# Six row pairs in place of seven by seven block products in a decoder layer's second feed-forward network, and a modulation slab's dot products moved

## The chip, the cores and the metric

The kernel runs on one core of a Trainium2 chip. The metric is the device time of one execution in microseconds. Before the change the median of three runs is 566.43 us (566.12 to 567.93).

## The reference, cut to what matters

One decoder layer over 256 tokens of width 1024, with a conditioning vector `c`: a feed-forward network, token mixing, a second feed-forward network and a final norm. All is float32.

```python
mod = c_act @ w_ada[l] + b_ada[l]
sh1, sc1, g1, sh2, sc2, g2, sh3, sc3, g3 = jnp.split(mod, N_MOD, axis=-1)
...
u = modulate(rmsnorm(h, norm_ff2[l]), sh3, sc3)
h = h + FFN_RES * g3[:, None, :] * swiglu(u, w_ff2_gate[l], w_ff2_up[l], w_ff2_down[l])
return rmsnorm(h, norm_final)
...
def swiglu(x, w_gate, w_up, w_down):
    return (jax.nn.silu(x @ w_gate) * (x @ w_up)) @ w_down
```

`w_ada` gives nine modulation slabs of 1024 columns each; the last, slab 8, is the gate `g3`. The hidden width is 2816, which is 22 blocks of 128.

## The kernel before

**Products.** Each float32 operand is split in two: ScalarE rounds it to a high part (`hi`), VectorE subtracts that from it (`lo`), and TensorE forms each product in three matmuls (high by high, high by low, low by high). Weight tiles are 128 by 1024. SP loads them into eight buffers (`raw`) in turn, so a load is issued when the tile eight places back has been read for the last time. The split parts have six buffers each (`hi`, `lo`). Every engine carries out its instructions in the order in which the program issues them (`InOrder`).

**The second feed-forward network** runs over the hidden blocks f0 to f21. *Step f n* (`gate_up`) makes block n: 48 matmuls of 256 columns, 24 for the gate and 24 for the up weights, into one PSUM bank; then ScalarE takes the silu (`sg`), VectorE the *product* with the up half (`m`), and both split it into the rows (`s`) that the down product reads. `Pipe.run` issues these two instructions and the splits of the next weight tiles behind the matmuls of the following step, so that five split tiles (`AHEAD4`) are kept ready.

**The down product** takes hidden blocks in pairs: *pair n* is f2n and f2n+1. A plain pair (`down`) has 48 matmuls of 256 columns. A pair in `QUARTERED` is instead multiplied as two by two blocks by Strassen's and Winograd's scheme, with seven block products (`sevenths`): the *first products* of pair n are three, issued behind step f2n+2, and the *last products* four, issued behind f2n+3. Each has three matmuls of 512 columns. Their seven sums stay in seven of the eight PSUM banks (`qbanks`) over all pairs. The scheme needs sums of weight blocks, which VectorE makes in two more `raw` tiles (`quarters`: one combination of 512 columns with the first tile, three with the second) and splits as well, and sums of hidden rows (`Halved.steps`, tile `wide`). Behind the last quartered pair VectorE puts the seven sums together (`put_together`, tile `of_token`), and 16 transposes bring the result into the accumulators of the plain pairs, which follow: the pairs ahead of `QUARTERED` through `down`, then pairs 9 and 10, which close the sum.

**The modulation slabs.** One *slab step* (`AdaQueue.step`) loads two tiles of `w_ada` and takes two dot products of 1024 columns on VectorE; four steps make a slab, and `ada_close` then adds the bias. `SLAB_AT` names the jobs behind which the four steps of slab 8 are issued: `("f", n)` is step f n, `(0, n)` and `(1, n)` are the first and the last products of pair n. Behind the last one, `as_row` writes two columns of the gate to DRAM and reads them back as a row over all partitions, by two DMAs of GpSimd (`rbs_dram`, `rbs`), and the same for the final norm's gain (`gqk`). The weight tiles of pairs 9 and 10 are multiplied by that row when they have been loaded (`Stream.load`, `raw<-raw,rbs`).

Of the kernel before, what the change touches and what calls it, by code (L numbers as in the profile page):

```python
# [30 lines left out]
LED = "g0 g0 g1 g0 g1 A g2 g4 g2 g3 g1 g2 g3 A g4 g3 g5 g6 g5 g7 g6 g4 g7 g6 g7 g5"  # L31
Q1_AT = (2, 4, 6, 7, 7, 10, 11, 11, 13, 16, 16, 17, 18, 22)
Q2_AT = (4, 9, 13)
SLAB_AT = ("f", 3), ("f", 4), (1, 4), (1, 7)
QUARTERED = range(2, 9)
HALF = 4 * P + 32
SW = S + 2
UP = 320
# [69 lines left out]
def hybrid_layer(ctx: ExitStack, tc: tile.TileContext, first, xT, tri_d, mask_d, rel_bias,  # L108
# [61 lines left out]
    def row(shape=(P, S), dt=F32, tag="r1", bufs=6):  # L170
        return wk.tile(list(shape), dt, tag=tag, name=name(tag), bufs=bufs)
# [54 lines left out]
    def mm(out_ap, bank_t, lhsT, rhs, stop=False):  # L226

        first = id(bank_t) not in opened
        i = ten.matmul(out_ap, lhsT, rhs, start=first, stop=stop, skip_group_check=True)
        last_mm[0] = i  # L230
        if first:
            opened[id(bank_t)] = (i, bank_t)
        else:
            tc.add_manual_dep(i.ins, opened[id(bank_t)][0].ins.name, DEP, reason="the bank's first matmul")
        return i
# [250 lines left out]
    def gated(b, t):  # L486

        sg = row(tag="sg", bufs=3)
        act.activation(sg, b[:, 0:S], AF.Silu)
        yield  # L490
        m = row(tag="m", bufs=3)
        vec.tensor_tensor(out=m, in0=sg, in1=b[:, S:2 * S], op=ALU.mult)
        yield
        split_rows(t[:, 0, :], t[:, 1, :], m)
        yield
# [20 lines left out]
    class Halved:  # L516
# [11 lines left out]
        def add(self, b, i=None):  # L528
            i = self.n if i is None else i
            self.n = max(self.n, i + 1)  # L530
            return self.steps(b, i) if i // 2 in QUARTERED else gated(b, self.place(i))

# [55 lines left out]
    def sevenths(n, todo, banks, hid):  # L588

        def run():  # L590
            ws = [stream.take() for _ in range(2)]
            for i, rows, w, half in todo:
                if i not in banks:
                    banks[i] = bank()
                for part, r in ((0, 0), (0, 1), (1, 0)):
                    mm(banks[i], banks[i], hid.at[n][rows][:, r], ws[w][part][:, half * HALF:half * HALF + 4 * P],
                       stop=(n == QUARTERED[-1] and part == 1))

        return run
# [15 lines left out]
    def gate_up(hid, u):  # L615
        def run():
            b = bank()
            for c in range(2):
                one_by_one(b, c * S, stream.take(), u)
            return lambda: all_of(hid.add(b))  # L620

        return run

    def down(n, banks, hid):
        def run():
            ws = [stream.take() for _ in range(2)]
            if not banks:
                banks.extend(bank() for _ in range(5))
            for j in range(KD):
                down_block(j, ws, banks, hid.tiles[n])  # L630

        return run
# [201 lines left out]
    for f in range(NF):  # L834
        stream.unit(("gu2", f), gu2[f])
        work2.append(("f", f))
        n, second = divmod(f - 2, 2)
        if n in QUARTERED:
            if not second:
# [3 lines left out]
    for n in range(NF // 2):  # L843
        if n not in QUARTERED:
            stream.unit(("dn2", n), dn2[n])
# [499 lines left out]
    def as_row(src, tag, bufs):  # L1345
        there, t = dr.tile([2, P], F32, name=f"{tag}_dram"), row(tag=tag, bufs=bufs)
        nc.gpsimd.dma_start(there.rearrange("i p -> p i"), src)
        nc.gpsimd.dma_start(t, bass.AP(tensor=there.tensor, offset=there[:, :].offset, ap=[[0, P], [1, 2 * P]]))
        return t
# [3 lines left out]
    def put_together():  # L1353
        of_token.extend([mid([P, D]), mid([P, D])])
        b, (u2, u3), (lo, hi) = qbanks, [row((P, 512), tag="wide", bufs=2) for _ in range(2)], (slice(0, 512), slice(512, D))
        act.activation(u2, b[1], AF.Copy)
        for to, x, y, op in ((of_token[0][:, lo], u2, b[2], ALU.add), (u2, u2, b[6], ALU.add),
                             (u3, u2, b[7], ALU.add), (of_token[1][:, lo], u3, b[4], ALU.subtract),
                             (of_token[1][:, hi], u3, b[5], ALU.add), (u2, u2, b[5], ALU.add),
                             (of_token[0][:, hi], u2, b[3], ALU.add)):  # L1360
            vec.tensor_tensor(out=to, in0=x, in1=y, op=op)

    for what, n in work2[3:]:
        pipe.run(gate_up(hid, u3) if what == "f" else sevenths(n, SEVENTHS[what], qbanks, hid))
        if (what, n) in SLAB_AT:
            slabs.step()
        if (what, n) == SLAB_AT[-1]:
            stream.gains, nf = as_row(mods[:, 8, 6:8], "rbs", 1), row((P, 8), tag="tiny", bufs=4)
            vec.tensor_copy(nf[:, :2], colt[:, C_NF + 6:C_NF + 8])
            nf_row = as_row(nf[:, :2], "gqk", 4)  # L1370
        if (what, n) == (1, QUARTERED[-1]):
            put_together()
# [3 lines left out]
    for t, js in ((0, range(4)), (1, range(4)), (1, range(4, 8)), (0, range(4, 8))):  # L1376
        for j in js:
# [4 lines left out]
            opened.setdefault(id(b), (x, b))  # L1382
    for n in range(QUARTERED[0]):
        pipe.run(down(n, dbanks, hid))
# [197 lines left out]
```

## Time and profile before

| | before |
|---|---|
| median of three runs | 566.43 us |
| profiled execution, its time | 569.2 us |
| profiled execution, span | 567.4 us |
| ScalarE busy | 317.2 us (56%) |
| GpSimd busy | 17.9 us (3%) |
| bytes moved | 141.99 MB, mean 250 GB/s |
| chain that ended last, TensorE's share | 84% |
| the same, VectorE's share | 10% |

A profile's rows give the start in microseconds from the span's start and the duration, then the engine (PE is TensorE, DVE VectorE, ACT ScalarE, POOL GpSimd, SP SyncE; a q behind it means its instruction queue), the operation, what it writes and reads by the program's tile names, and the shape. Almost all instructions have line 133, since a helper issues them. In brackets stands how long the engine was idle before, and which engine and tile released it. A row with xN joins N instructions.

### The profile page before, as it was taken

Reading aid. Unit: us, or ns where it says so; the run is one execution under the profiler, and the core shown is the slowest. Engines: PE = TensorE matmul, PEld = TensorE weight load, DVE = VectorE, ACT = ScalarE, POOL = GpSimd, SP = SyncE. Lnnn points to the kernel's source line nnn. Section 1 sums busy time; section 2 is a strip of 40 time slices with the busy share of each in tenths; the row PEclk is TensorE's granted clock in tenths of the full one; section 3 lists DMA queues with packets and bytes.
Section 4 is the critical chain, followed back from the end, with each engine's and each line's share of the span. In section 5 each row is a group of like instructions: output and inputs, shape, how many; then the busy total and the mean of one; then the engine's idle time right before and its main releaser. Section 6 shows DMA issues by size and latency. Waiting matters only on the chain.

```text
span 567.4 us, 11461 instructions
## 1 busy us (share of the span) xinstructions
PE 552.8 (97%) x4531; PEld 537.8 (95%) x4531; DVE 485.4 (86%) x781; ACT 317.2 (56%) x531; POOL 17.9 (3%) x39
## 2 busy tenths in 40 slices
PE   7999999999999999999999999999899989998996
PEld 6999999999999999989999999999898979997996
DVE  6999897888887896999999888899888998987845
ACT  5557754444444678944955344676465554663524
POOL 1000030000000100000010000000000000001000
PEclk9999999999999999999999999999999989998999
DMA  8999799999998446545597879817746665659602
GB/s 326 409 408 408 236 354 392 407 342 344 322 383 263 152 142 230 176 151 181 191 351 293 319 263 305 261 39 236 246 154 219 197 219 177 216 191 216 215 2 74
DMA packets 40541, 141.99 MB, mean 250 GB/s; under 512 B 4740, under 2 KB 6248, under 8 KB 40488
## 3 DMA queue, kind: packets, MB, share of 16 engines
q1 hardware_dynamic: 39720, 139.55, 70.9%
q0 software_dynamic: 336, 0.80, 0.5%
q10 hardware_dynamic: 432, 0.92, 0.5%
q8 instruction: 35, 0.57, 0.4%
q14 instruction: 18, 0.15, 0.1%
HBM read 140.19 MB, written 1.06 MB: 249 GB/s over the span
## 4 chain that ended last, share of the span: by engine, by line
PE 84%; DVE 10%; issue 3%; ACT 1%; DMA 1%; POOL 0%; POOLq 0%; DVEq 0%; SPq 0%; ACTq 0%
PE b L133 84%; DVE lo L133 4%; DVE raw L133 3%; DVE m L133 1%; DMA b<-in_first 1%; DVE wide L133 1%; DVE s L133 1%; DVE n L133 1%; DVE ub L133 0%; ACT s L133 0%; ACT hi L133 0%; DVE sg L133 0%; ACT sg L133 0%; POOL tiny L435 0%; POOLq L1577 0%
## 5 line engine op out<-in xcount | busy, mean ns | idle before, releaser
L133 PE MATMUL b<-ub,hi 128*128 128x256 f32 (+1 forms) x1920 | 323.6, 280 | 5.7 <-DVE m L133 5.7
L133 PEld LDWEIGHTS b<-ub,hi 128*128 128x128 f32 x1920 | 284.5, 190 | 8.9 <-DVE m L133 7.9
L133 DVE TENSOR_TENSOR lo<-raw,hi 128x1024 fp32r<-128x1024 f32 (+2 forms) x204 | 236.3, 1192 | 31.4 <-ACT hi L133 30.8
L133 PE MATMUL b<-ub,lo 128*128 128x256 f32 (+1 forms) x960 | 246.6, 278 | 0.0
L133 ACT ACTIVATE hi<-raw 128x1024 fp32r<-128x1024 f32 (+2 forms) x204 | 202.3, 1029 | 39.8 <-DMA raw<-in_first 16.0
L133 PEld LDWEIGHTS b<-ub,lo 128*128 128x128 f32 x960 | 172.7, 190 | 0.0
L133 PE MATMUL b<-s,hi 128*128 128x256 f32 x720 | 123.5, 276 | 0.0
L133 PEld LDWEIGHTS b<-s,hi 128*128 128x128 f32 x720 | 108.4, 188 | 0.0
L133 PE MATMUL b<-s,lo 128*128 128x256 f32 x360 | 99.4, 276 | 0.0
L133 ACT ACTIVATE s<-m 128x256 fp32r<-128x256 f32 (+1 forms) x52 | 20.8, 403 | 104.6 <-DVE m L133 104.6
L133 DVE SCALAR_TENSOR_TENSOR raw<-raw,cact 128x1024 f32<-128x1024 f32 (+1 forms) x64 | 75.8, 1219 | 0.0
L133 PEld LDWEIGHTS b<-s,lo 128*128 128x128 f32 x360 | 67.6, 188 | 0.0
L133 ACT ACTIVATE sg<-b 128x256 f32<-128x256 f32 x46 | 17.1, 379 | 39.9 <-PE b L133 38.9
L133 PE MATMUL b<-hi,s 128*128 128x512 f32 (+1 forms) x114 | 34.1, 385 | 1.7 <-ACT s L133 1.1
L133 DVE TENSOR_TENSOR s<-m,s 128x256 fp32r<-128x256 f32 (+1 forms) x52 | 20.9, 405 | 16.5 <-ACT s L133 16.3
L133 PEld LDWEIGHTS b<-hi,s 128*128 128x128 f32 x114 | 19.8, 190 | 5.6 <-ACT s L133 1.5
L133 ACT ACTIVATE s<-b 128x512 f32<-128x512 f32 (+5 forms) x38 | 14.7, 437 | 17.6 <-PE b L133 16.7
L133 DVE TENSOR_TENSOR m<-sg,b 128x256 f32<-128x256 f32 x43 | 17.7, 416 | 5.1 <-ACT sg L133 5.0
L133 PE MATMUL b<-lo,s 128*128 128x512 f32 (+1 forms) x57 | 21.4, 387 | 0.0
L133 PE MATMUL b<-hi,ub 128*128 128x264 f32 (+1 forms) x96 | 16.7, 322 | 0.0
L133 ACT ACTIVATE sq<-b 128x256 f32<-128x256 f32 x24 | 9.1, 406 | 11.4 <-DVE b L133 9.3
L133 DVE SCALAR_TENSOR_TENSOR b<-b,mods,b 128x256 f32<-128x256 f32 x24 | 10.4, 478 | 5.9 <-PE b L133 5.9
(152 smaller groups left out, 361.2 us busy)
## 6 DMA issues: line engine op xcount, KB each, us to landing
raw<-in_gu SPq DMA_DIRECT2D x72, 512.0 KB, 5.5
raw<-in_ada SPq DMA_DIRECT2D x56, 512.0 KB, 5.8
raw<-in_dn SPq DMA_DIRECT2D x44, 512.0 KB, 6.7
raw<-in_win SPq DMA_DIRECT2D x24, 512.0 KB, 4.5
raw<-in_first SPq DMA_DIRECT2D x16, 513.0 KB, 8.3
raw<-in_first SPq DMA_DIRECT2D x16, 512.0 KB, 8.1
raw<-in_gbr SPq DMA_DIRECT2D x16, 512.0 KB, 6.4
raw<-in_wout SPq DMA_DIRECT2D x8, 512.0 KB, 5.5
```

The source lines that it names most:

```text
L133: x = getattr(self.engine, op)(*args, **kw)
```

## The change

The first quartered pair is 3 in place of 2: six pairs are left, and pair 2 becomes a third plain pair in front of pairs 9 and 10. The four steps of slab 8 stand behind f3, f5, f20 and f21 in place of f3, f4, pair 4's last products and pair 7's last products. `as_row` goes with the last of them.

```diff
-SLAB_AT = ("f", 3), ("f", 4), (1, 4), (1, 7)
-QUARTERED = range(2, 9)
+SLAB_AT = ("f", 3), ("f", 5), ("f", 20), ("f", 21)
+QUARTERED = range(3, 9)
```

On VectorE ahead of the quartered pairs, from the split behind product f3 on, there stand before (`raw<-raw` without a second input is a weight combination, `raw,gemv` a dot product of a slab step):

```order
L133 TENSOR_TENSOR lo_5303<-raw_5300,hi_5302 128x2x512
L133 TENSOR_TENSOR raw_5310<-raw_5306 128x512
L133 TENSOR_TENSOR lo_5313<-raw_5306,hi_5312 128x512
L133 SCALAR_TENSOR_TENSOR raw_5316,gemv<-raw_5316,cact 128x1024
L133 SCALAR_TENSOR_TENSOR raw_5319,gemv<-raw_5319,cact 128x1024
L133 TENSOR_TENSOR m_5373<-sg_5371,b_5245 128x256
L133 TENSOR_TENSOR s_853_5375<-m_5373,s_853_5375 128x128
L133 TENSOR_TENSOR raw_5310<-raw_5308,raw_5310 128x512
L133 TENSOR_TENSOR raw_5378<-raw_5308,raw_5306 128x512
L133 TENSOR_TENSOR raw_5378<-raw_5310,raw_5308 128x512
L133 TENSOR_TENSOR lo_5383<-raw_5308,hi_5382 128x2x512
L133 TENSOR_TENSOR lo_5389<-raw_5386,hi_5388 128x2x512
```

and of the change at the same place:

```order
L133 TENSOR_TENSOR lo_5303<-raw_5300,hi_5302 128x2x512
L133 TENSOR_TENSOR lo_5309<-raw_5306,hi_5308 128x2x512
L133 TENSOR_TENSOR m_5364<-sg_5362,b_5245 128x256
L133 TENSOR_TENSOR s_847_5361<-m_5364,s_847_5361 128x256
L133 TENSOR_TENSOR lo_5371<-raw_5368,hi_5370 128x2x512
L133 TENSOR_TENSOR lo_5377<-raw_5374,hi_5376 128x2x512
L133 SCALAR_TENSOR_TENSOR raw_5380,gemv<-raw_5380,cact 128x1024
L133 SCALAR_TENSOR_TENSOR raw_5383,gemv<-raw_5383,cact 128x1024
L133 TENSOR_TENSOR m_5437<-sg_5435,b_5312 128x256
L133 TENSOR_TENSOR s_847_5361<-m_5437,s_847_5361 128x256
L133 TENSOR_TENSOR lo_5444<-raw_5441,hi_5443 128x2x512
L133 TENSOR_TENSOR raw_5451<-raw_5447 128x512
```

Product f4 (`m` from `b_5245`) has moved ahead of the slab step, product f5 (`b_5312`) follows it, and the weight combinations of the first quartered pair begin behind that, two steps later.

On VectorE behind the quartered pairs, from the splits that follow the put-together on, there stand before (products f20 and f21, scalings by `rbs`):

```order
L133 TENSOR_TENSOR lo_6817<-raw_6814,hi_6816 128x2x512
L133 TENSOR_TENSOR lo_6823<-raw_6820,hi_6822 128x2x512
L133 TENSOR_TENSOR m_6878<-sg_6876,b_6765 128x256
L133 TENSOR_TENSOR s_1117_6875<-m_6878,s_1117_6875 128x256
L133 TENSOR_TENSOR raw_6887<-raw_6887,rbs_6568 128x256
L133 TENSOR_TENSOR lo_6885<-raw_6882,hi_6884 128x2x512
L133 TENSOR_TENSOR raw_6894<-raw_6894,rbs_6568 128x256
L133 TENSOR_TENSOR lo_6892<-raw_6887,hi_6891 128x2x512
L133 TENSOR_TENSOR m_6970<-sg_6968,b_6826 128x256
```

and of the change, from the second dot product of the first of its two slab steps there on:

```order
L133 SCALAR_TENSOR_TENSOR raw_6750,gemv<-raw_6750,cact 128x1024
L133 TENSOR_TENSOR m_6805<-sg_6803,b_6686 128x256
L133 TENSOR_TENSOR s_1098_6802<-m_6805,s_1098_6802 128x256
L133 TENSOR_TENSOR lo_6812<-raw_6809,hi_6811 128x2x512
L133 TENSOR_TENSOR lo_6818<-raw_6815,hi_6817 128x2x512
L133 SCALAR_TENSOR_TENSOR raw_6821,gemv<-raw_6821,cact 128x1024
L133 SCALAR_TENSOR_TENSOR raw_6824,gemv<-raw_6824,cact 128x1024
L133 TENSOR_TENSOR mods<-gemv,bada 128x8
...
L133 TENSOR_TENSOR m_6911<-sg_6909,b_6753 128x256
L133 TENSOR_TENSOR s_1098_6802<-m_6911,s_1098_6802 128x256
L133 TENSOR_TENSOR raw_6920<-raw_6920,rbs_6830 128x256
L133 TENSOR_TENSOR lo_6918<-raw_6915,hi_6917 128x2x512
```

The slab is now closed (`mods<-gemv,bada`) shortly ahead of product f21 and of the first scaling by its row; before, it was closed ahead of f18's product. The split that stands behind the first scaling (`lo_6918`) is that of the second tile of plain pair 2; in its place before (`lo_6885`) stood that of the second tile of plain pair 1.

## The prediction

> **What bounds the kernel now.** I read the page's busy times first, then TensorE's timeline over the second feed-forward network, then the clock in windows, then VectorE's timeline, then the DMA landings.
>
> ```profile
> PE 552.8 (97%) x4531; PEld 537.8 (95%) x4531; DVE 485.4 (86%) x781; ACT 317.2 (56%) x531; POOL 17.9 (3%) x39
> ```
>
> TensorE is the bound by its share, so time is saved only where it waits, runs slowly, or gets less to do. Its timeline names every wait in the stage (start, length, instruction, and in brackets the idle time ahead of it and its releaser):
>
> ```profile
> 407.27 0.62 PE L133 MATMUL b<-hi,s 128*128 128x512 f32 x2
> 409.22 0.49 PE L133 MATMUL b<-hi,s 128*128 128x512 f32 x1 [1.10 <-ACT s L133]
> 410.29 0.66 PE L133 MATMUL b<-hi,s 128*128 128x512 f32 x1 [0.57 <-DVE s L133]
> 429.89 0.51 PE L133 MATMUL b<-ub,hi 128*128 128x256 f32 x2 [0.79 <-DVE m L133]
> 464.11 0.51 PE L133 MATMUL b<-ub,hi 128*128 128x256 f32 x2 [2.20 <-DVE m L133]
> 516.35 0.80 PE L133 MATMUL b<-ub,hi 128*128 128x256 f32 x2 [2.66 <-DVE m L133]
> ```
>
> The first row is the start of pair 2's first products, right behind step f6. The waits add up to 7.3 us. The last three open f9, f13 and f19: seven banks hold the block products, so a step gets the one bank left only when VectorE's product `m` of the step before has read it. Three of these places also cost clock (PE, PEld, DVE, ACT, POOL busy, then granted clock, DMA share, GB/s):
>
> ```profile
> 410.00:420.00 10.00, 9.71 (x60) 8.93 (x61) 8.35 (x11) 6.79 (x10) 0.00 (x0) 0.83 0.44 145
> 460.00:470.00 10.00, 7.80 (x46) 7.12 (x45) 8.97 (x13) 4.05 (x6) 0.00 (x0) 0.83 0.77 251
> 510.00:520.00 10.00, 7.34 (x42) 6.61 (x41) 8.93 (x15) 3.64 (x5) 1.48 (x2) 0.83 1.01 282
> ```
>
> 0.83 over 10 us is 1.7 us lost each, behind idle times of 1.67 (two pieces), 2.20 and 2.66 us; behind the 0.79 there is no such loss.
>
> **TensorE's own prices.** Undisturbed rows, the starts of pair 3's last products, f10, pair 4's first products, f11, pair 5's first products, pair 8's last products, the transposes and the first plain down product:
>
> ```profile
> 435.53 0.62 PE L133 MATMUL b<-hi,s 128*128 128x512 f32 x2
> 438.29 0.40 PE L133 MATMUL b<-ub,hi 128*128 128x256 f32 x2
> 443.75 0.62 PE L133 MATMUL b<-hi,s 128*128 128x512 f32 x2
> 445.88 0.51 PE L133 MATMUL b<-ub,hi 128*128 128x256 f32 x2
> 459.68 0.62 PE L133 MATMUL b<-hi,s 128*128 128x512 f32 x2
> 523.47 0.62 PE L133 MATMUL b<-hi,s 128*128 128x512 f32 x2
> 537.18 1.91 PE L133 MATMUL b<-ident,s 128*128 128x128 f32 x16
> 538.84 0.48 PE L133 MATMUL b<-s,hi 128*128 128x256 f32 x2
> ```
>
> Last products take 2.76, a step 5.46, first products 2.1, a whole pair (443.75 to 459.68) 15.93 with its small bank waits. A plain pair at the end has 48 matmuls of 256 columns, as a step has: 5.45. The sixteen transposes take 1.66.
>
> **The change, ahead of the stage.** VectorE's rows from product f3 on, which are the same up to 398.59 in both kernels:
>
> ```profile
> 396.74 0.41 DVE L133 TENSOR_TENSOR m<-sg,b 128x256 f32<-128x256 f32 x1
> 398.59 1.23 DVE L133 TENSOR_TENSOR lo<-raw,hi 128x1024 fp32r<-128x1024 f32 x1 [0.53 <-ACT hi L133]
> 399.73 0.68 DVE L133 TENSOR_TENSOR raw<-raw 128x512 f32<-128x512 f32 x1
> 400.94 1.22 DVE L133 SCALAR_TENSOR_TENSOR raw<-raw,cact 128x1024 f32<-128x1024 f32 x1
> 403.23 0.42 DVE L133 TENSOR_TENSOR m<-sg,b 128x256 f32<-128x256 f32 x1
> 408.30 0.41 DVE L133 TENSOR_TENSOR m<-sg,b 128x256 f32<-128x256 f32 x1
> 420.18 0.41 DVE L133 TENSOR_TENSOR m<-sg,b 128x256 f32<-128x256 f32 x1
> 429.43 0.41 DVE L133 TENSOR_TENSOR m<-sg,b 128x256 f32<-128x256 f32 x1
> ```
>
> Prices: a split of 1024 columns 1.14 (398.59 to 399.73), combination plus half split 1.21, a slab step (two dot products) 2.29, product to next split 1.85. New order: two splits from 398.59, product f4 at 400.87; two splits, the slab step now behind f5, product f5 at 407.29; one split, combination and half split, product f6 at 411.49. From there the rows are those of before, one pair on: 403.23 to 408.30 is 5.07, so product f7 falls at 416.56, which is 8.26 later than its counterpart, f5 (408.30). TensorE, with f7 and f8 in a row and no products of pair 2, starts pair 3's first products at 407.27 + 2 x 5.46 = 418.19, which is 10.92 later than pair 2's. So VectorE is 2.7 us less late, and the waits of 1.10 and 0.57 go with their lost clock.
>
> A remainder stays. Product f9 falls at 420.18 + 8.26 = 428.44, and f10 starts 0.46 behind it (429.43 to 429.89), at 428.9. TensorE then reaches f11 at 428.9 + 5.46 + 2.1 = 436.5, but product f10 falls at 437.69 and f11 starts at 438.15: **a wait of 1.65 us in place of several**. It equals the 1.67 that cost clock before, so I charge 1.7 more (below: 0, as behind the 0.79).
>
> [...]
>
> **Inside the stage** both slab steps are gone, and with them the waits of 2.20 and 2.66 and their clock; four pairs run undisturbed. f19 starts at 438.15 + 4 x 15.93 = 501.87, and f21 ends at 501.87 + 5.46 + 2.76 + 2 x 5.46 = 521.0, where before the transposes start at 537.18: 16.2 us earlier. Pair 2 comes back as a plain pair, 5.45. **Gross gain 10.7 us, or 9.0 with the clock charge.** The combinations and extra splits that pair 2 loses (VectorE and ScalarE) are within these positions.
>
> **Behind the stage** comes the new risk. Slab 8 now ends here, its last gate goes by two GpSimd DMAs to DRAM and back as a row, and the four last weight tiles are scaled by that row. VectorE's rows of before (slab step, product f19, put-together, two splits, product f20, first scaling) and GpSimd's (write, read):
>
> ```profile
> 510.85 1.22 DVE L133 SCALAR_TENSOR_TENSOR raw<-raw,cact 128x1024 f32<-128x1024 f32 x1
> 524.09 0.42 DVE L133 TENSOR_TENSOR m<-sg,b 128x256 f32<-128x256 f32 x1 [0.88 <-ACT sg L133]
> 533.04 2.35 DVE L133 TENSOR_TENSOR lo<-raw,hi 128x1024 fp32r<-128x1024 f32 x2
> 535.31 0.41 DVE L133 TENSOR_TENSOR m<-sg,b 128x256 f32<-128x256 f32 x1
> 536.55 0.42 DVE L133 TENSOR_TENSOR raw<-raw,rbs 128x256 f32<-128x256 f32 x1
> ...
> 513.93 0.76 POOL L1347 DMA_DIRECT2D rbs_dram<-mods  x1 [139.30 <-DVE tiny L133]
> 526.14 0.58 POOL L1348 DMA_DIRECT2D rbs<-rbs_dram  x1 [10.73 <-ACT hi L133]
> ```
>
> Product f19 comes 0.62 behind its step (523.47 to 524.09): 507.33 + 0.62 = 507.95. Product f20 comes 11.22 later plus one slab step: 521.46. Then 1.85, two splits, and the last slab step at 525.6; the write is issued 3.08 behind its start (510.85 to 513.93), at 528.7. If the write lands after W and the read, issued 0.5 later, after R, the row is there at 529.2 + W + R. VectorE stands still on the first scaling until then, and queued behind that is the split of plain pair 2's second tile, ready 1.6 after the row (scaling 0.35, split 1.14, hand-over). TensorE needs it in the third plain product: 521.0 + 1.66 + 2 x 5.45 = 533.57, sixth matmul at 534.1. **The wait is W + R - 3.3.** The cover is exactly these two plain products; everything behind is refilled within the third product. The dot products themselves cost nothing here, since products f20 and f21 hold no bank that is waited for. Their weight loads stand between the others in SP's queue; each waits for the buffer eight tiles back, and those of the last slab step get theirs from splits that end before the put-together, about 512, 13 us before use, so no load is late (landings below). GpSimd's queue holds nothing else here.
>
> W and R are bounded by these landings (issue, size, us to landing) and two windows:
>
> ```profile
> rbs_dram<-mods POOLq DMA_DIRECT2D x1, 1.0 KB, 11.7
> rbs<-rbs_dram POOLq DMA_DIRECT2D x1, 128.0 KB, 6.9
> rdram<-wide POOLq DMA_DIRECT2D x1, 6.0 KB, 5.3
> out<-b SPq DMA_DIRECT2D x5, 128.0 KB, 1.8
> raw<-in_gu SPq DMA_DIRECT2D x1, 512.0 KB, 3.2
> ...
> 525.00:526.00 1.00, 1.00 (x6) 0.79 (x5) 0.47 (x2) 1.00 (x2) 0.00 (x0) 1.00 1.01 119
> 530.00:531.00 1.00, 1.00 (x11) 1.00 (x10) 0.90 (x2) 0.21 (x1) 0.00 (x0) 1.00 1.03 406
> ```
>
> Before, write and read ran against the loads of eight down tiles, and the engines, fully busy, moved 119 GB/s beside the write against 406 later. Now the last load is issued when the first of the two splits ahead of the last slab step frees its buffer (eight buffers in turn), about 524.5, and should land by 529: the queues are nearly empty. So W lies between 1.8 (the small outputs) and 11.7, R between 1.8 and 6.9. I take 5.3 for W, the other small write by GpSimd, and for R the quiet load's 3.2 less 384 KB at 406 GB/s (0.95) plus GpSimd's 0.58: 2.8. The wait is 8.1 - 3.3 = 4.8, and 1.7 of clock behind it.
>
> [...] No quiet GpSimd DMA is in this trace, and the three here lie at 5.3 and above.
>
> **Sum.** 16.2 - 5.45 - 1.7 - 4.8 - 1.7 = 2.5 us gained. The profiled execution took 569.2 (span 567.4), so 566.7 by its measure; the median shown is 566.43, so **563.9**.
>
> **Rivals.** (1) **The row comes early**: W + R at most 6.0, because nothing competes. At 1.8 + 1.8 the wait is 0.3 with no clock loss: 566.43 - 8.7 = 557.7. For it speaks the empty queue; against it, that the write moves elements of 4 bytes. (2) **Slower: the row's write is slow by itself.** For it: bandwidth collapsed exactly while it ran, as if 512 single elements (two writes) held the engines. With W 11.7 and R 2.8 the wait is 11.2: 566.43 - 9.0 + 11.2 + 1.7 = 570.3; with R 6.9 too, 574.4. It decides from W + R = 10.6 on. (3) **The relief fails**: the step ahead moves, but VectorE still reaches f11 late; that is the 1.65, already charged, and without its clock loss all times are 1.7 lower.
>
> **Chances.** Early row (under 561.8) 0.25; forecast's band, W + R from 6.0 to 10.6 (561.8 to 566.4), 0.47; slow write 0.28. A measurement tells 0.3%, 1.7 us. Of the middle band 0.30 is faster by that, with rival 1 0.55; of the slow case 0.07 stays within 0.3%, so same 0.24, slower 0.21. The range leaves out the ends of both rivals: 558.4 to 570.5.
>
> **What would show it.** Right: no wait above 0.5 us ahead of pair 3's first products; one of about 1.65 at f11, with a window at 0.83 behind it; none at f13 to f19; transposes some 14 to 16 us earlier; a wait in the third plain product, released by VectorE's `lo` behind a scaling by `rbs`. Wrong: the landings of `rbs_dram` and `rbs` sum to far from 8.1, or waits appear between f12 and f19.

## The result, and the profile after

The changed kernel takes 571.65 us (median of six runs) against 567.95 for the kernel before in the same sets of runs: **ratio 1.0069, 95% interval 1.0045 to 1.0093**, slower. The forecast was 563.9, faster. The profiled execution took 571.14 with a span of 569.0, against 567.4 before, so 1.6 us more span. The medians lie further apart, 3.7 us. The profiled execution before has a mean granted clock of 0.991; of thirteen executions of the same kernel in a later set of runs, seven have 0.997 and spans of 564.1 to 566.1. So the profile that the prediction reads had lost more clock than about half of these executions.

The stage itself did what was forecast. TensorE's waits in the changed kernel, with the start of the sixteen transposes between them:

```profile
429.07 0.51 PE L133 MATMUL b<-ub,hi 128*128 128x256 f32 x2 [0.30 <-DVE m L133]
438.32 0.51 PE L133 MATMUL b<-ub,hi 128*128 128x256 f32 x2 [1.47 <-DVE m L133]
521.29 1.91 PE L133 MATMUL b<-ident,s 128*128 128x128 f32 x16
543.88 0.58 PE L133 MATMUL b<-s,lo 128*128 128x256 f32 x1 [9.21 <-DVE lo L133]
```

The five waits of before (7.3 us) have become two in the stage (f10 and f11, 1.8 us), f11 starts at 438.32 (forecast 438.15), and the transposes stand 15.9 us earlier than before (537.18). Then the third plain product stops for 9.21 us. The windows show the clock, in the column behind POOL's busy time, at f11 and around that stop:

```profile
430.00:440.00 10.00, 8.54 (x66) 7.82 (x65) 8.60 (x13) 6.51 (x9) 0.00 (x0) 1.00 0.54 184
534.00:544.00 10.00, 0.79 (x7) 0.59 (x6) 1.74 (x3) 1.06 (x1) 1.13 (x2) 0.76 0.18 26
544.00:550.00 6.00, 6.00 (x31) 6.00 (x32) 5.46 (x7) 3.18 (x3) 0.00 (x0) 0.55 0.02 4
```

The 1.47 us at f11 cost no clock. Behind the long stop the clock was 0.55 over 6 us, which is 2.7 us lost. The chain that ended last says what the stop waited for, in order of time (start, length, what):

```profile
528.96 8.20 DMA rbs_dram<-mods
537.20 0.52 issue
537.72 4.52 DMA rbs<-rbs_dram
...
542.61 1.23 DVE lo L133
543.88 20.06 PE b L133 x151
```

The gate's write is issued at 528.96 (forecast 528.7), lands after 8.2, its read after 4.5. The split at 542.61, that of plain pair 2's second tile, is what TensorE needs. The forecast wait, W + R - 3.3, gives 8.2 + 4.5 - 3.3 = 9.4 with the landings as they were; measured are 9.2. The balance is 15.9 - 5.45 - 9.2 - 2.7 = -1.5, and the span says -1.6.

### The profile page after: what moved, and what is told of

Same layout as the page of the kernel before. It is cut to its first block, busy times and chain, and to the rows that moved or that the text cites. A ratio compares the mean times of both kernels' runs of the same rounds, so it can differ in the third digit from the quotient of the medians.

```text
span 569.0 us, 11505 instructions
## 1 busy us (share of the span) xinstructions
PE 551.8 (97%) x4558; PEld 538.4 (95%) x4558; DVE 479.6 (84%) x770; ACT 314.9 (55%) x528; POOL 17.8 (3%) x39
## 4 chain that ended last, share of the span: by engine, by line
PE 88%; DVE 5%; DMA 3%; issue 2%; ACT 1%; POOL 0%; POOLq 0%; DVEq 0%; SPq 0%; ACTq 0%
PE b L133 88%; DVE lo L133 2%; DMA rbs_dram<-mods 1%; DVE raw L133 1%; DMA b<-in_first 1%; DMA rbs<-rbs_dram 1%; ACT hi L133 1%; DVE s L133 1%; DVE wide L133 1%; DVE m L133 0%; POOL tiny L435 0%; ACT s L133 0%; POOLq L1577 0%; DVE b L133 0%; DVE tiny L133 0%
## 5 line engine op out<-in xcount | busy, mean ns | idle before, releaser
L133 PE MATMUL b<-ub,hi 128*128 128x256 f32 (+1 forms) x1920 | 319.7, 278 | 1.8 <-DVE m L133 1.8
L133 PEld LDWEIGHTS b<-ub,hi 128*128 128x128 f32 x1920 | 281.1, 188 | 4.8 <-DVE m L133 3.9
L133 PE MATMUL b<-s,hi 128*128 128x256 f32 x752 | 131.3, 279 | 0.0
L133 PEld LDWEIGHTS b<-s,hi 128*128 128x128 f32 x752 | 115.2, 191 | 0.0
L133 PE MATMUL b<-s,lo 128*128 128x256 f32 x376 | 105.3, 280 | 9.2 <-DVE lo L133 9.2
L133 PEld LDWEIGHTS b<-s,lo 128*128 128x128 f32 x376 | 71.8, 191 | 9.4 <-DVE lo L133 9.4
L133 PE MATMUL b<-hi,s 128*128 128x512 f32 (+1 forms) x100 | 28.8, 376 | 0.0
L133 PEld LDWEIGHTS b<-hi,s 128*128 128x128 f32 x100 | 17.1, 188 | 2.6
L133 PE MATMUL b<-lo,s 128*128 128x512 f32 (+1 forms) x50 | 18.2, 376 | 0.0
```

Source lines behind the costliest of these rows:

```text
L133: x = getattr(self.engine, op)(*args, **kw)
```

## The experiments

All start from the changed kernel unless said otherwise. Some profiled executions came to the second network 1.2 to 1.6 us later than the changed kernel did (f11 at 439.6 to 439.9), so waits and distances are compared, and spans only with that in mind.

### Is the row's DMA all that took the gain?

The row is made on TensorE, behind the first plain product, and the tiles are scaled just ahead of their split:

```diff
-            stream.gains, nf = as_row(mods[:, 8, 6:8], "rbs", 1), ...
+            nf = ...
     for n in range(QUARTERED[0]):
+        pipe.depth = AHEAD4 - 1 if n == 0 else AHEAD4
         pipe.run(down(n, dbanks, hid))
+        if n == 0:
+            pg, stream.gains = bank(), row(tag="rbs", bufs=1)
+            for i in range(2):
+                ten.transpose(pg[:, blk(i)], mods[:, 8, 6 + i:7 + i].to_broadcast([P, P]), ident)
+            act.activation(stream.gains, pg[:, :S], AF.Copy)
```

> The changed kernel, but the gate's row is made by two transposes on TensorE behind the first plain product and a copy on ScalarE, with the scaling just ahead of each split; no DMA is in that chain. If the wait for the row is all that took the gain: no wait above 0.7 us in the plain products, no half clock there, span 569.0 - 9.2 - 2.7 + 0.5 = 557.6, ratio to before about 0.983. Rival (VectorE is late behind the put-together anyway, since two slab steps were added there): a wait of several us by VectorE's splits stays, span over 562.

Span 559.6, median 562.09, ratio 0.9898 (0.9854 to 0.9941). No wait is left in the plain products; a new one stands behind them. TensorE's row and two of VectorE's:

```profile
543.22 0.51 PE L133 MATMUL b<-s,hi 128*128 128x256 f32 x2 [1.99 <-DVE b L133]
...
541.55 1.23 DVE L133 TENSOR_TENSOR lo<-raw,hi 128x1024 fp32r<-128x1024 f32 x1 [1.17 <-ACT hi L133]
542.69 0.87 DVE L133 SCALAR_TENSOR_TENSOR b<-b,mods,b 128x256 f32<-128x256 f32 x2
```

VectorE reads the two finished output blocks (542.69) only behind the last split, and that came late because each tile was scaled, rounded and subtracted one after the other. So the wait of 9.2 us and its 2.7 of lost clock are gone with the row's DMA, and 2.0 of a new wait came in, a fault of this version, with 0.4 for the two transposes: the span is 9.4 us shorter than the changed kernel's. The next one scales a tile ahead, and prepares no tile of pair 9 before the row is there:

```diff
-            while self.todo and len(self.ready) < n:
+            while self.todo and len(self.ready) < n and not (self.todo[0][0] in self.scaled and self.gains is None):
```

> As the run that makes the row by two transposes, but the later weight tiles are scaled one tile ahead of their split again, and no tile of pair 9 is prepared before the row is there. If the 2.0 us wait of that run came from VectorE reaching the two output blocks late behind a chain of scaling, rounding and subtraction of 2.7 us a tile: that wait goes, span 557.6 to 558, ratio to before about 0.982. If it came from elsewhere, span stays 559.6.

Span 557.5, median 559.72, **ratio 0.9846 (0.9819 to 0.9872)**. TensorE's only waits:

```profile
429.10 0.51 PE L133 MATMUL b<-ub,hi 128*128 128x256 f32 x2 [0.29 <-DVE m L133]
438.35 0.50 PE L133 MATMUL b<-ub,hi 128*128 128x256 f32 x2 [1.41 <-DVE m L133]
```

The 2.0 us wait is gone, as expected of the chain. By the profiled spans this is the gross gain of the prediction: 567.4 - 557.5 = 9.9 us, where its terms without any wait for the row and without a clock charge gave 10.7. By the medians it is 8.5 us (568.18 to 559.72), since many executions of the kernel before lose less clock than the profiled one. The moved steps and the plain pair were sized about rightly; the rest is the row.

### The two halves of the change

Six pairs and the step behind f5, but the last two steps back in the stage:

```diff
-SLAB_AT = ("f", 3), ("f", 5), ("f", 20), ("f", 21)
+SLAB_AT = ("f", 3), ("f", 5), (1, 4), (1, 7)
```

> The changed kernel with the last two slab steps back behind the last products of pairs 4 and 7; six row pairs and the slab step behind f5 remain. If the step ahead of the stage and the steps within it add up as in the prediction: f11 starts near 438.3, waits of 2.2 and 2.7 us with their half clock come back in the stage, the transposes start near 537.2 - 7.6 = 529.6, no wait for the row, span 567.4 - 7.6 + 5.45 = 565.3. Rival (the third plain pair costs more than 5.45, or the first half gains nothing): span 567 or over.

Span 564.8, median 565.65, ratio 0.9955 (0.9933 to 0.9977). The waits of before are back in the stage, and none behind it:

```profile
439.71 0.50 PE L133 MATMUL b<-ub,hi 128*128 128x256 f32 x2 [1.41 <-DVE m L133]
457.94 0.50 PE L133 MATMUL b<-ub,hi 128*128 128x256 f32 x2 [2.15 <-DVE m L133]
508.50 0.79 PE L133 MATMUL b<-ub,hi 128*128 128x256 f32 x2 [2.61 <-DVE m L133]
529.14 1.91 PE L133 MATMUL b<-ident,s 128*128 128x128 f32 x16
```

From f11 to the transposes it is 89.4 us (before: 445.88 to 537.18, 91.3). The 1.9 us less are mostly the half clock that the 2.15 did not bring here. The span is 2.6 us shorter than before, although this execution came to f11 1.4 us late; less the 1.9 us of luck with the clock, the front half gains 2.1 us, as its terms said (f11 7.6 earlier, less the plain pair's 5.45). The other half, seven pairs as before with the moved steps and the row on TensorE:

```diff
-SLAB_AT = ("f", 3), ("f", 5), ("f", 20), ("f", 21)
-QUARTERED = range(3, 9)
+SLAB_AT = ("f", 3), ("f", 4), ("f", 20), ("f", 21)
+QUARTERED = range(2, 9)
```

> Seven row pairs as before, the slab's steps behind f3, f4, f20 and f21, and the row by two transposes as in the run with tiles scaled ahead: the moved steps without the dropped pair. By the prediction's terms the first wait and half clock ahead of pair 2 come back (f11 at 445.9 in place of 438.2, 7.6 us), one plain pair (5.45) goes, and with only two plain products the scaled tiles come about 0.5 us late: span 557.7 + 7.6 - 5.45 + 0.5 = 560.4. If the dropped pair were worth nothing or a loss: 558 or less.

Span 560.9, median 562.87, ratio 0.9902 (0.9875 to 0.9929). The first waits are there again,

```profile
409.58 0.51 PE L133 MATMUL b<-hi,s 128*128 128x512 f32 x1 [1.07 <-ACT s L133]
410.64 0.50 PE L133 MATMUL b<-hi,s 128*128 128x512 f32 x1 [0.56 <-DVE s L133]
446.14 0.51 PE L133 MATMUL b<-ub,hi 128*128 128x256 f32 x2
```

and f11 starts at 446.14, 7.8 us later than with six pairs (438.35). Dropping the pair is worth 560.9 - 557.5 = 3.4 us, the plain pair already paid. Of these 1.0 is a late wait for VectorE behind the plain products, which only the seven-pair version has (at 544.54); the pair alone is worth about 2.4, or 7.8 - 5.45.

### What makes the write take 8 us

Only the gate's write and read under way, the gain's row having been made long before:

```diff
+    nf = row((P, 8), tag="tiny", bufs=4)
+    vec.tensor_copy(nf[:, :2], colt[:, C_NF + 6:C_NF + 8])
+    nf_row = as_row(nf[:, :2], "gqk", 4)
     for what, n in work2[3:]:
```

> The changed kernel, but the final norm's gain is turned into a row at the start of the second feed-forward network, so that only the gate's write and read are under way behind f21. Theory A (each GpSimd DMA has a latency of its own, whatever else is in its queue): the gate's write still lands after 8.2 us and its read after 4.5, the wait in the third plain product stays 9.2 and the span 569.0. Theory B (the 512 single elements of the two writes hold each other up): the write lands in about 4.8, half of what lies behind its first 1.5 us, the wait falls to about 5.5 and the span to 564 to 565.

Median 571.32, ratio 1.0049 (1.0033 to 1.0066). The landings (issue, size, us) hardly moved, and TensorE's wait fell by 0.7 only, about as much as the two landings together (12.7 to 12.1):

```profile
rbs<-rbs_dram POOLq DMA_DIRECT2D x1, 128.0 KB, 4.2
rbs_dram<-mods POOLq DMA_DIRECT2D x1, 1.0 KB, 7.9
...
544.40 0.58 PE L133 MATMUL b<-s,lo 128*128 128x256 f32 x1 [8.54 <-DVE lo L133]
```

With half the elements under way the write takes 7.9 in place of 8.2: theory B falls, theory A stands. Next, the write issued earlier, beside loads (`slabs.step(SLAB_AT.count((what, n)))` lets a place stand twice):

```diff
-SLAB_AT = ("f", 3), ("f", 5), ("f", 20), ("f", 21)
+SLAB_AT = ("f", 3), ("f", 5), ("f", 20), ("f", 20)
```

> The changed kernel with both last slab steps behind f20, so that the gate is closed one step of VectorE earlier. Theory A (fixed latencies): the write is issued 4.5 us earlier, lands 8.2 later, the wait in the third plain product falls from 9.2 to 4.7, span near 564. Theory C (the landing depends on what else is loaded): the write now runs beside loads of the last down tiles, lands later than 8.2, up to 11.7, and the wait is 5 to 8, span 565 to 568.

Span 564.5, median 566.73, ratio 0.9973 (0.9954 to 0.9991):

```profile
rbs<-rbs_dram POOLq DMA_DIRECT2D x1, 128.0 KB, 3.6
rbs_dram<-mods POOLq DMA_DIRECT2D x1, 1.0 KB, 9.0
...
539.38 0.58 PE L133 MATMUL b<-s,lo 128*128 128x256 f32 x1 [5.01 <-DVE lo L133]
```

Write and read together take 12.6, as in the changed kernel (12.7); the loads added 0.8 to the write at most. So the chain has a near-fixed length, and an issue 4.4 us earlier took 4.2 us off the wait; the 5.0 us left lie close to theory A's 4.7 and at the lower edge of theory C's 5 to 8. Whose length is it? First the same elements by ScalarE's queue:

```diff
-            stream.gains, nf = as_row(mods[:, 8, 6:8], "rbs", 1), ...
+            stream.gains, nf = as_row(mods[:, 8, 6:8], "rbs", 1, nc.scalar), ...
```

> The changed kernel with the gate's write and read issued from ScalarE's queue in place of GpSimd's. Theory A1 (the latency belongs to GpSimd's way of issuing a DMA): write and read land in about 2 us each, as the outputs that ScalarE and SP issue do (1.7 to 2.1), the wait in the third plain product is under 1.5 us, span 558 to 560. Theory A2 (the latency belongs to single 4-byte elements written to DRAM, whoever issues them): the write still lands after 7 to 8 us, the read after 2 to 3, the wait is 6 to 8, span 565 to 567.

Span 569.3, median 570.76, ratio 1.0038 (1.0019 to 1.0057). The landings, and the packets of ScalarE's queue (q10) between 529 and 530 us:

```profile
rbs<-rbs_dram ACTq DMA_DIRECT2D x1, 128.0 KB, 5.1
rbs_dram<-mods ACTq DMA_DIRECT2D x1, 1.0 KB, 8.6
out<-b ACTq DMA_DIRECT2D x1, 128.0 KB, 1.8
...
q10 hardware_dynamic: 272, 0.00, 14.7%
```

The write, issued at 528.43, had its packets (272, which fits 256 elements and 16 more) recorded before 530, and still landed at 537.0. Who issues it makes little difference (8.6 against 8.2): A1 falls. Of A2 the write holds, but the read took 5.1 in place of 2 to 3, so TensorE waited 9.4 us. The output `out<-b` goes to DRAM by the same queue from 128 partitions too, in rows of 1 KB, and lands in 1.8: neither that queue nor 128 partitions made that write slow. Then one line of 1 KB written from one partition in place of 256 elements, by GpSimd as before (the row then holds other values):

```diff
-        nc.gpsimd.dma_start(there.rearrange("i p -> p i"), src)
+            line = row(tag="rbl", bufs=1)
+            vec.tensor_scalar(line[0:1], cact[0:1, :S], mods[0:1, 8, 6:7], None, op0=ALU.mult)
+            nc.gpsimd.dma_start(there.rearrange("i p -> (i p)")[None, :], line[0:1])
```

> The run with the gate's write alone, but what GpSimd writes is one line of 1 KB from one partition (16 runs of 64 bytes) in place of 256 elements of 4 bytes; the row then holds other values, so the gate of two output blocks is left out. Theory A1 (GpSimd's way of issuing): the write still lands after 7 to 8 us. Theory A2 (single elements): it lands in 2 to 4 us, the wait falls from 8.5 to 3 to 5.

One execution: 562.67 us, span 560.5. The write lands even earlier than A2 said, and so the wait is shorter:

```profile
rbs<-rbs_dram POOLq DMA_DIRECT2D x1, 128.0 KB, 3.2
rbs_dram<-rbl POOLq DMA_DIRECT2D x1, 1.0 KB, 1.6
...
537.91 0.39 PE L133 MATMUL b<-s,lo 128*128 128x256 f32 x1 [1.56 <-DVE lo L133]
```

As many bytes to the same place land in 1.6 us; W + R - 3.3 gives 1.5 for the wait, and measured are 1.56. **It is the writing in elements of 4 bytes that took about 8 us here (7.9 to 8.6)**, with next to no loads beside it, from either queue, with one such write under way or two. This run also has one partition as source in place of 128; that this is not the reason rests on `out<-b` above. Why the read takes from 3.2 us (here) to 5.1, no run separates.

### The remaining wait at f11

From the version with the row on TensorE, the step behind f5 moved behind f20, and the transposes behind the second plain product:

```diff
-SLAB_AT = ("f", 3), ("f", 5), ("f", 20), ("f", 21)
+SLAB_AT = ("f", 3), ("f", 20), ("f", 20), ("f", 21)
```

> The row by two transposes with tiles scaled ahead, and the slab step behind f5 moved behind f20 as well (two there, one behind f21); the transposes stand behind the second plain product. If the wait of 1.4 us at f11 is VectorE's lateness from the step behind f5, it goes together with the 0.3 at f10, and the plain products still cover the 2.3 us that VectorE is later there: span 557.5 - 1.7 = 555.8. Rival (the cover behind the stage is spent): f11's wait goes but waits by VectorE's splits or output blocks of 1.5 to 3 us come in the plain products, span 557 to 559.

Span 556.3, median 558.61, **ratio 0.9839 (0.9810 to 0.9868)**. TensorE has one wait left in the second network:

```profile
539.92 0.51 PE L133 MATMUL b<-s,hi 128*128 128x256 f32 x2 [1.02 <-DVE b L133]
```

The waits at f10 and f11 (1.7) are gone and 1.0 came back behind the plain products, so both theories were partly right. It is the fastest of all by its median; its interval overlaps that of the version before it (0.9819 to 0.9872).

## Why the prediction was wrong

- **What bounds the kernel, and the step ahead of the stage: right.** f11 fell 0.2 us from its forecast, with a wait of 1.47 against 1.65, and the front half alone gains about the 2 us that its terms give.
- **The clock charge at f11: wrong.** 1.7 us were charged because 1.67 idle us had cost that much before. No clock was lost behind 1.37 to 1.47 us at f11 in any profile that has this wait. By luck this error hid part of the one below.
- **Inside the stage: right.** No wait at f13 to f19. The transposes came 15.9 us earlier (forecast 16.2), and seven pairs against six confirm the price of the dropped pair (f11 7.8 us later, forecast 7.6).
- **The wait for the row: the mechanism right, its size the step that failed.** Place, cover (3.3 us) and formula held to 0.2 us. But W was taken as 5.3, "the other small write by GpSimd", and R as 2.8 from a quiet load. Measured are 8.2 and 4.5, so the wait was 9.2 in place of 4.8: 2.9 us by the write and 1.7 by the read. The choice rested on the landing of 11.7 being due to competing loads. The runs show that loads are the smaller part of it. Two such writes beside the stage's loads take 11.3 and 11.7, and without or with few loads it is 7.9 to 9.0; in one line it is 1.6. In the run that makes the gain's row at the start of the network, the read follows that single write after 8.9 us, and the gate's behind the stage after 8.4. The row chosen as nearest, `rdram<-wide`, writes four lines of 1.5 KB, so it was near in issuer and far in what mattered. What made the read 4.5 in place of 2.8 stays open. The slow-write rival had this mechanism ("the write moves elements", 0.28), and its threshold, W + R = 10.6, is passed by the measured 12.7.
- **The clock behind the long wait: mis-sized.** 2.7 us in place of 1.7; these two errors, with the missing charge at f11, make the difference: 4.4 + 1.0 - 1.7 = 3.7 us of wait and clock, and 0.4 in the rest, against the 4.1 between 2.5 gained and 1.6 lost by the profiles.
- **The sum: a profile's gain taken off a median.** The gain was read from an execution of 569.2 us with three stretches at half clock and taken off a median of 566.43. So 563.9 counts as gained some clock that the executions at the median had not lost. The spans of the two profiles are 1.6 us apart and the medians 3.7; of the 2.1 between, 1.2 are the profiled execution before (569.2) lying above its median (567.95). The last 1.5 of the 7.7 us from 563.9 to 571.65 are that median itself, 567.95 in place of 566.43.
- **The lower end of the range.** 558.4 stands for a wait of 1.0, which is W + R = 4.3: an author's estimate that no run shows. With the write by elements behind the stage W + R was 12.1 to 13.7, and with the write in one line 4.8.

## What to carry to other kernels

When work is moved out of a full stage, follow what hangs on its last result: here a slab step's 2.3 us of VectorE could be moved at no cost, and a chain of two dependent DMAs behind it did not. Price a DMA by a row of the same element size, not of the same number of bytes (1 KB landed after 8.2 us in elements and after 1.6 in one line); if none is in the trace, the range has to hold the slowest row whole. Turning a column into a row needs no trip through DRAM: two transposes of a broadcast column did it, with 0.4 us of TensorE. And time lost to the clock in one profile is not a fixed price of a wait (behind 2.20 us of it the kernel before lost 1.7 to the clock, behind 2.15 the front half's run lost none): look at several executions before it is counted as a gain.

## What the runs showed of the hardware

**The time of the element write lies behind its packets.** ScalarE's element write had its 272 packets recorded before 530 us (above), and no packet of any queue is recorded between 530.4 and its landing at 537.0. By GpSimd it looks alike, though there both kinds of write leave 32 packets, which do not show the single elements. These are the changed kernel's packets from 530 to 531 us, those of the gate's write, and from 532 to 537 (the 32 in between belong to the gain's write, issued 0.8 us later), and behind them those of the write in one line from 532 to 532.5:

```profile
DMA packets 32, 0.00 MB, mean 1 GB/s; under 512 B 32, under 2 KB 32, under 8 KB 32
...
DMA packets 0, 0.00 MB, mean 0 GB/s; under 512 B 0, under 2 KB 0, under 8 KB 0
...
DMA packets 32, 0.00 MB, mean 2 GB/s; under 512 B 32, under 2 KB 32, under 8 KB 32
```

The gate's write by elements lands at 537.2, over 6 us behind its packets; the write in one line, issued at 531.00, lands 1.6 us later at 532.6, about half a us behind its own. What passes in the 6 us the trace doesn't say, and it stays open.

**Half clock lasted 3.41 us each time in the kernel before, and three times that in the changed kernel.** Before, it begins at 410.46, 465.07 and 516.27. The distances are 54.61 and 51.20, which is 16 and 15 times 3.413. Behind the long stop of the changed kernel it lasted from 539.14 to 549.38, 10.24 us or three times 3.413, of which 5.5 us were work: the 2.7 us lost. The rows below count steps of that length from where half clock begins in the same trace, and so show in which step a wait lies (behind the step's length stands TensorE's busy time, and the granted clock is third from the end). First the kernel before, two of its half clocks, each with the step ahead of it:

```profile
407.04:410.46 3.42, 1.75 (x9) 0.97 (x8) 3.09 (x8) 0.94 (x2) 0.00 (x0) 1.00 0.84 279
410.46:413.87 3.41, 3.41 (x12) 2.88 (x13) 3.02 (x4) 2.26 (x4) 0.00 (x0) 0.50 0.12 49
461.66:465.07 3.41, 1.21 (x10) 0.96 (x9) 2.69 (x4) 0.98 (x2) 0.00 (x0) 1.00 0.78 274
465.07:468.48 3.41, 3.41 (x19) 3.41 (x18) 3.10 (x3) 2.17 (x3) 0.00 (x0) 0.50 0.64 203
```

Then the front half's run with its waits of 2.15 and 2.61:

```profile
453.43:456.84 3.41, 2.36 (x12) 1.63 (x10) 3.41 (x6) 0.39 (x1) 0.00 (x0) 1.00 0.93 255
456.84:460.25 3.41, 2.31 (x19) 2.32 (x20) 2.38 (x4) 2.33 (x4) 0.00 (x0) 1.00 0.82 267
460.25:463.67 3.42, 3.42 (x32) 3.42 (x31) 3.42 (x5) 1.34 (x2) 0.00 (x0) 1.00 0.78 204
504.63:508.04 3.41, 1.26 (x6) 0.70 (x4) 3.34 (x8) 0.00 (x0) 1.48 (x2) 1.00 0.75 217
508.04:511.45 3.41, 2.95 (x14) 2.95 (x15) 2.40 (x5) 2.97 (x4) 0.00 (x0) 0.50 0.98 328
```

and f11 of the changed kernel, whose steps are counted back from 539.14:

```profile
436.75:440.16 3.41, 1.95 (x16) 1.84 (x16) 2.38 (x5) 1.86 (x3) 0.00 (x0) 1.00 0.63 216
440.16:443.57 3.41, 3.41 (x32) 3.41 (x31) 3.41 (x4) 1.82 (x3) 0.00 (x0) 1.00 0.60 217
```

In the front half's run the wait of 2.15 lies across two steps, with 1.05 us idle in the first and 1.10 in the second, and the clock stayed at 1.00 in both and in the next. Of the wait of 2.61, 2.15 us lie in one step, and the next ran at 0.50. So of the steps shown, those with 1.67, 2.15 and 2.20 us idle were followed by half clock, and those with 1.05, 1.10 and 1.47 (f11) were not. The length of the whole wait doesn't order them: 1.67 and 2.20 cost clock in the kernel before, while 2.15 here and the 1.99 in the first run with the row on TensorE (1.00 from 540 to 555) cost none. What sets the 3.41 us, and how much idle time it takes elsewhere, no run shows. The charge of 1.7 at f11 had only the 1.67 of before to go by, and measured is none.

The thirteen executions of the kernel before have mean granted clocks from 0.989 to 0.997. One stretch at half clock takes 0.003 off the mean (1.7 of 567 us), so they differ by what some two or three such stretches cost, an estimate from these numbers. Why they differ is not shown, since one execution alone has its trace kept.
